# A hybrid attention, state-space and expert block: waits inside an expert pair taken out, and the second norm computed in another way

## The chip, the cores and the metric

The kernel runs on one core of one Trainium2 chip. The metric is the device time of one execution in microseconds (us), as the median of several runs. The profile was taken from one more execution of the same program.

## The reference, cut to what matters

256 tokens of width 2048 pass through a mixer (attention beside a state-space model), a layer norm, a mixture of 32 experts and a second layer norm. The change lies in the experts and in the second norm. Each token goes to its two best experts; all 32 experts are needed, and the weights of one are three matrices of 2048 x 512 numbers of 4 bytes.

```python
h = layer_norm(DEEPNORM_ALPHA * x + mix, ln1_g, ln1_b)
...
def expert_block(args):
    tok, e = args
    xb = h[tok]
    return (jax.nn.silu(xb @ w_gate[e]) * (xb @ w_up[e])) @ w_down[e]
...
out = jnp.zeros((n, d), jnp.float32).at[buf_tok].add(y.reshape(buf_len, d) * buf_w[:, None])
...
return layer_norm(DEEPNORM_ALPHA * h + ffn, ln2_g, ln2_b)

def layer_norm(x, g, b):
    mu = xf.mean(-1, keepdims=True)
    var = jnp.square(xf - mu).mean(-1, keepdims=True)
    return ((xf - mu) * lax.rsqrt(var + NORM_EPS) * g + b).astype(x.dtype)
```

## The kernel before, in words

The instructions of each engine stand in the order in which the code is written; nothing reorders them. The first 425 us hold the mixer, the first norm and the router. Then the experts follow, two at a time, in 16 pairs (0 to 15; the last is `LASTP`). Each expert has room for 64 tokens, and the two experts of a pair fill the two halves of TensorE's columns. Tokens beyond 64 for one expert would be treated in the overflow loop behind the pairs (`tc.For_i`), whose count comes from the data; with these inputs the profile shows no pass of it.

A pair does the following. TensorE multiplies the gathered tokens `xg` by the gate weights (`p_gate`) and the up weights (`p_up`), in four pieces each. `hidden` then lets ScalarE take the silu, VectorE multiply by the up half, TensorE transpose the result (`p_ht`) and ScalarE copy it into the tile `xg` (`aT`). `gather` makes the tokens of the next pair by matmuls with a one-hot matrix `S` (`p_g`); it has four parts. `weights_t` makes the routing weights of the pair (`p_sw`), which ScalarE copies to `swT` and `wsl`. The down products (`p_dn`) come in four chunks of 512 columns; `weighted` splits each into a high and a low part for the fast fp32r matmul (ScalarE writes the one, VectorE the other), and `combine` adds them to the sums of all tokens through a matmul with `swT` (`p_co`). In the last pair all weights come in half-size pieces and the down products in eight chunks of 256 columns.

Products in PSUM lie in banks that are used in turn by tag: "acc" has three, "s" and "t" two each, "o" one. `p_ht` and `p_sw` share "o"; `p_g` uses "t"; `p_dn` and `p_co` use "acc" (the last pair's `p_dn` uses "t").

The weights come through one queue of SyncE into a ring of slots, in program order. `ring_take` gives a piece to the matmuls and puts its slot on the list of free ones, and `ring_fill` writes loads into the free slots, oldest first; on the chip such a load waits until the matmuls that read the slot are done. A load also waits until the eighth load before it has landed, since there are eight DMA semaphores. Late in the program other tiles take slots from the same list.

`split_rows2` and `rows2` bring g and b of the second norm into two tiles whose 128 rows are all alike. Behind the overflow loop `norm_stats` aggregates the statistics, and `normed`, `scaled` and `shifted` apply the norm in eight units (two halves of the tokens by four column ranges), each followed by its store.

Of the kernel before, what the change touches and what calls it, by code (L numbers as in the profile page):

```python
# [10 lines left out]
F32 = mybir.dt.float32  # L11
# [59 lines left out]
def block_kernel(ctx: ExitStack, tc: tile.TileContext, I: dict, out: bass.AP):  # L71
# [878 lines left out]
    def ring_load(n=1):  # L950
        for i in range(ring["next"], min(ring["next"] + n, len(items))):
            nm, src, e, q = items[i]
            if second(i):
                at, t = ring["open"]
            else:
                at = ring["free"].pop(0)
                t = slot(at, "w" + nm)
                ring["open"] = at, t
            ring["next"] = i + 1
            ring["tiles"][nm, e, q] = t, at  # L960
            if nm == "row":
                nc.sync.dma_start(t[:8, :512], I["ln2_rows"])
# [185 lines left out]
    def weighted(py, wsl, i):  # L1148
# [4 lines left out]
        dve.scalar_tensor_tensor(lo, py, wsl, f(hi), op0=OP.mult, op1=OP.subtract)  # L1153
        return hi, lo

    def combine(swT, ys, lo, w, fin=None, init=False):
        s = slice(lo, lo + w)
        for a in range(2):
            pc = bank("acc", "p_co")[:, :w]
            for y, part in enumerate(ys):  # L1160
                pe.matmul(pc, swT[:, a * P:(a + 1) * P], part, start=(y == 0), stop=(y == 1))  # L1161
            if init:
                dve.tensor_copy(acc[a][:, s], pc)
            else:
                dve.tensor_add(acc[a][:, s], acc[a][:, s], pc)  # L1165
            if fin:
                for h in range(lo, lo + w, 256):
                    dve.bn_stats(st2[:, a, h // 256], acc[a][:, h:h + 256])

    def sums_first(lo, w):  # L1170

# [3 lines left out]
        return pcs  # L1175

    def combine_last(pcs, swT, ys, lo, w):
        for y, part in enumerate(ys):
            for a in range(2):
                pe.matmul(pcs[a], swT[:, a * P:(a + 1) * P], part, start=False, stop=(y == 1))  # L1180
# [73 lines left out]
        dve.tensor_scalar(base, base, float(P), float(CAP), op0=OP.mult, op1=OP.add)  # L1254


    gb = {}

    def split_rows2():

        raw = ring_take("row", -1, None)[:8, :512]
        gb["rows"] = mo.tile([64, 512], F32R, name="gb2", tag="gb1")
        gb["one"] = mo.tile([64, 8], F32R, name="one2")
        dve.memset(f(gb["rows"]), 0.0)
        dve.tensor_add(gb["one"], ident[:64, 0:8], ident[:64, 32:40])
        act.copy(gb["rows"][:8], raw)
        dve.tensor_tensor(gb["rows"][32:40], raw, f(gb["rows"][:8]), op=OP.subtract)

    def rows2(j):
        if j % 4 == 0:  # L1270
            gb[j // 4] = slot(ring["free"].pop(0), f"row{j // 4}")
        p = bank("acc", "p_row")
        pe.matmul(p, gb["one"][:40, j:j + 1].to_broadcast([40, P]), gb["rows"][:40], start=True, stop=True)
        act.copy(gb[j // 4][:, 512 * (j % 4):512 * (j % 4) + 512], p)

    st2 = mo.tile([P, 2, 8, 6], F32, name="st2")
    one_hots(0)
# [12 lines left out]
    for j in range(8):  # L1290
        besides.setdefault((LASTP, "g" if j < 2 else "u", (3, 3, 0, 0, 0, 1, 1, 1)[j]), []).append((rows2, j))
    for pr in range(NE // 2):
        pg, pu = bank("s", "p_gate"), bank("s", "p_up")
        for nm, pp in (("g", pg), ("u", pu)):
# [26 lines left out]
        aT = next(hid)  # L1321
        if pr < LASTP:
            weights_t(pr)
        late = None
        for i, (c, lo, w) in enumerate(DOWN_LAST if pr == LASTP else DOWN):
            tl = [ring_take("d", 2 * pr + u, (lo, w)) for u in range(2)]
            py = bank("t" if pr == LASTP else "acc", "p_dn")[:, :w]
            for q in range(4):
                for u in range(2):
                    pe.matmul(py[64 * u:64 * u + 64, :], aT[:, q, 64 * u:64 * u + 64], tl[u][:, q], start=(q == 0),  # L1330
                              stop=(q == 3), skip_group_check=True)
            ring_fill()
# [70 lines left out]
    mean, rstd, nmr = norm_stats(st2, "2")  # L1403
    dve.scalar_tensor_tensor(nmr, mean, -1.0, rstd, op0=OP.mult, op1=OP.mult)  # L1404
    units = [(a, slice(c * 512, (c + 1) * 512)) for a in range(2) for c in range(4)]

    def normed(i):
        a, s = units[i]
        act.activation(acc[a][:, s], acc[a][:, s], AF.Identity, scale=rstd[:, a:a + 1], bias=nmr[:, a:a + 1])

    def scaled(i):
        a, s = units[i]
        v = acc[a][:, s]
        if i % 2 == 0:
            dve.scalar_tensor_tensor(v, v, mean[:, a:a + 1], gb[0][:, s], op0=OP.subtract, op1=OP.mult)  # L1415
# [3 lines left out]
    def shifted(i):
        a, s = units[i]  # L1420
        v = acc[a][:, s]
        if i % 2 == 0:
            dve.scalar_tensor_tensor(v, v, rstd[:, a:a + 1], gb[1][:, s], op0=OP.mult, op1=OP.add)  # L1423
        else:
            pool.tensor_tensor(v, v, gb[1][:, s], op=OP.add)  # L1425

    def store(i):
        a, s = units[i]
        nc.sync.dma_start(out[0][a * P:(a + 1) * P, s], acc[a][:, s])

    for i in (1, 3, 5, 7):
        normed(i)
    for fn, i in ((scaled, 0), (shifted, 0), (scaled, 1), (shifted, 1), (scaled, 3), (shifted, 3), (scaled, 2), (scaled, 5),
                  (shifted, 5), (shifted, 2), (scaled, 7), (shifted, 7), (scaled, 4), (shifted, 4), (scaled, 6),
                  (shifted, 6)):
        fn(i)
# [10 lines left out]
def _laid_out(inputs):  # L1447
# [22 lines left out]
    a["ln2_rows"] = np.concatenate([flat("ln2_g"), flat("ln2_b")]).reshape(8, 512)  # L1470
# [22 lines left out]
```

## Time and profile before

| | |
|---|---|
| median of 3 runs | 1393.09 us (1392.07 to 1394.43) |
| the profiled execution: its own time | 1393.33 us |
| its span, first to last instruction | 1391.6 us |
| TensorE busy in the span | 94% |
| VectorE, ScalarE, GpSimd busy | 37%, 26%, 11% |
| read from HBM | 468.79 MB |

The span is 1.73 us shorter than the time of the execution it belongs to. Shares are means over stages with different limits, and TensorE's matmuls are pipelined, so that 94% doesn't say which engine or transfer sets the end of a stage.

### The profile page before, as it was taken

How to read it: one execution, taken by the hardware profiler on the slowest of the kernel's cores; microseconds unless marked ns; L12 is line 12 of the kernel's file. 1: busy time of each engine (PE TensorE's matmuls, PEld its weight loads, DVE VectorE, ACT ScalarE, POOL GpSimd, SP SyncE). 2: the span in 40 equal slices, each digit the busy share in tenths (PEclk: the TensorE clock that was granted, in tenths of full speed). 3: DMA queues.
4: the chain of work that ended last, by engine and by line, in shares of the span. 5: the costliest groups of instructions: out<-in, count | busy, mean ns of one | idle time of the engine just before them, and what ended most of it. 6: DMA issues, size and time to landing. Idle time of an engine off the chain costs nothing. (4 is left out here: it accounts for less than half of the span.)

```text
span 1391.6 us, 18135 instructions
## 1 busy us (share of the span) xinstructions
PE 1312.2 (94%) x7347; PEld 758.6 (55%) x7347; DVE 513.8 (37%) x1085; ACT 357.2 (26%) x687; POOL 154.1 (11%) x78
## 2 busy tenths in 40 slices
PE   7998999999999999999999999999999999999994
PEld 6778899997885434344344443444434444344432
DVE  6757676468833323131121312213122131221207
ACT  5554566455424102011010111101111011110112
POOL 2533233333520000000000000000000000000001
PEclk9999999999999999999999999999999999999997
DMA  8752334435798899999999999999999999999981
GB/s 314 288 177 91 122 103 141 152 122 212 302 412 342 350 391 421 421 421 421 421 421 421 421 421 421 421 421 421 421 421 421 421 421 421 421 420 421 407 325 61
DMA packets 70692, 472.10 MB, mean 339 GB/s; under 512 B 8510, under 2 KB 8766, under 8 KB 17102
## 3 DMA queue, kind: packets, MB, share of 16 engines
q1 hardware_dynamic: 70016, 470.75, 83.6%
q8 instruction: 59, 0.97, 0.3%
q10 hardware_dynamic: 590, 0.17, 0.1%
q14 instruction: 27, 0.22, 0.0%
HBM read 468.79 MB, written 2.10 MB: 338 GB/s over the span
## 5 line engine op out<-in xcount | busy, mean ns | idle before, releaser
L1330 PE MATMUL p_dn<-wd,xg 128*64 128x512 f32 (+1 forms) x1088 | 241.4, 587 | 14.9 <-DVE work L1153 14.3
L1300 PE MATMUL p_gate<-wg,xg 128*64 128x512 f32 x1024 | 225.9, 596 | 0.0
L1300 PE MATMUL p_up<-wu,xg 128*64 128x512 f32 x1024 | 222.9, 592 | 0.0
L222 POOL TENSOR_TENSOR w_lo<-raw,w_hi 128x1024 fp32r<-128x1024 f32 x52 | 141.4, 2721 | 258.4 <-ACT w_hi L221 245.8
L1189 DVE TENSOR_TENSOR xg<-xg,p_up 128x512 f32<-128x512 f32 x16 | 11.0, 688 | 394.1 <-ACT xg L1188 394.1
L1300 PEld LDWEIGHTS p_up<-wu,xg 128*64 128x64 f32 x1024 | 73.3, 137 | 145.5 <-issue 141.9
L1330 PEld LDWEIGHTS p_dn<-wd,xg 128*64 128x64 f32 x1088 | 73.7, 139 | 142.7 <-issue 108.0
L1300 PEld LDWEIGHTS p_gate<-wg,xg 128*64 128x64 f32 x1024 | 71.6, 137 | 143.7 <-issue 136.2
L1153 DVE SCALAR_TENSOR_TENSOR work<-p_dn,wsl,work 128x512 fp32r<-128x512 f32 (+1 forms) x68 | 48.9, 719 | 269.8 <-ACT work L1152 269.8
L1125 PEld LDWEIGHTS p_g<-S,hp 128*128 128x128 f32 x1024 | 120.8, 194 | 28.2 <-issue 26.0
L1125 PE MATMUL p_g<-S,hp 128*128 128x128 f32 x1024 | 127.2, 281 | 0.9 <-DVE cnt L1278 0.9
L221 ACT CAST w_hi<-raw 128x1024 fp32r<-128x1024 f32 (+1 forms) x112 | 109.0, 1027 | 36.9 <-issue 9.1
L1152 ACT ACTIVATE work<-p_dn,wsl 128x512 fp32r<-128x512 f32 (+1 forms) x68 | 45.2, 664 | 278.2 <-PE p_dn L1330 275.1
L1425 POOL TENSOR_TENSOR sum<-sum,row 128x512 f32<-128x512 f32 x4 | 6.7, 1691 | 972.3 <-DVE sum L1417 972.3
L310 PE MATMUL p_acc<-xh,w_hi 128*128 128x256 f32 x384 | 112.5, 293 | 0.0
L1188 ACT ACTIVATE xg<-p_gate 128x512 f32<-128x512 f32 x16 | 9.6, 597 | 391.7 <-PE p_up L1300 391.7
L312 PE MATMUL p_acc<-xl,w_hi 128*128 128x256 f32 x384 | 109.6, 285 | 0.0
L313 PE MATMUL p_acc<-xh,w_lo 128*128 128x256 f32 x384 | 109.6, 285 | 0.0
L222 DVE TENSOR_TENSOR w_lo<-raw,w_hi 128x1024 fp32r<-128x1024 f32 (+1 forms) x60 | 78.2, 1309 | 33.1 <-ACT w_hi L221 33.0
L1165 DVE TENSOR_TENSOR sum<-sum,p_co 128x512 f32<-128x512 f32 (+1 forms) x130 | 79.7, 650 | 9.5 <-PE p_co L1161 9.5
L1161 PE MATMUL p_co<-work,swT 128*128 128x512 f32 (+1 forms) x268 | 76.7, 408 | 0.0
L310 PEld LDWEIGHTS p_acc<-xh,w_hi 128*128 128x128 f32 x384 | 74.8, 195 | 0.7
(382 smaller groups left out, 1465.2 us busy)
## 6 DMA issues: line engine op xcount, KB each, us to landing
wg<-in_w_gate SPq DMA_DIRECT2D x120, 1024.0 KB, 15.3
wu<-in_w_up SPq DMA_DIRECT2D x120, 1024.0 KB, 17.7
wd<-in_w_down SPq DMA_DIRECT2D x120, 1024.0 KB, 11.7
raw<-in_w_dense SPq DMA_DIRECT2D x52, 1024.0 KB, 4.9
wg<-in_w_gate SPq DMA_DIRECT2D x16, 512.0 KB, 10.8
wu<-in_w_up SPq DMA_DIRECT2D x16, 512.0 KB, 10.2
wd<-in_w_down_last SPq DMA_DIRECT2D x16, 512.0 KB, 10.2
cw<-in_cmp_w SPq DMA_DIRECT2D x4, 1024.0 KB, 6.8
```

The source lines that it names most:

```text
L221: act.copy(hi[:, ks, :w], raw)
L222: eng.tensor_tensor(lo[:, ks, :w], raw, f(hi[:, ks, :w]), op=OP.subtract)
L310: pe.matmul(dst, hi[:, k, s], xk(xh, kt), start=(first and k == 0 and j % 2 == 0), stop=False, skip_group_check=True)
L312: pe.matmul(dst, hi[:, k, s], xk(xl, kt), start=False, stop=False, skip_group_check=True)
L313: pe.matmul(dst, lo[:, k, s], xk(xh, kt), start=False, stop=(last and k == 3), skip_group_check=True)
L1125: pe.matmul(at(k), hpm[a][:, 4 * c + k], S[:, a], start=(a == 0), stop=(a == 1))
L1152: act.activation(hi, py, AF.Copy, scale=wsl)
L1153: dve.scalar_tensor_tensor(lo, py, wsl, f(hi), op0=OP.mult, op1=OP.subtract)
L1161: pe.matmul(pc, swT[:, a * P:(a + 1) * P], part, start=(y == 0), stop=(y == 1))
L1165: dve.tensor_add(acc[a][:, s], acc[a][:, s], pc)
L1300: pe.matmul(pp[64 * u:64 * u + 64, :], xg[:, kk, 64 * u:64 * u + 64], tl[u][:, k], start=(kk == 0), stop=(kk == KT - 1), skip_group_check= ...
L1330: pe.matmul(py[64 * u:64 * u + 64, :], aT[:, q, 64 * u:64 * u + 64], tl[u][:, q], start=(q == 0), stop=(q == 3), skip_group_check=True)
```

## The change: what it does

Inside a pair, three things move or change place. `weights_t` of a pair is written into its up products (behind the second piece) instead of ahead of its down products. The transposes `p_ht` stand between the first two parts of the gather instead of behind them. The second and third down product use the banks "t" instead of "acc".

In the last pair the weighted down product is kept whole in fp32 (`weighted_whole`, no high and low part, one fp32 matmul instead of two fp32r ones), `g` is multiplied onto the sums as soon as each chunk is summed (`vg`), and the statistics, a small matmul (`p_rl`) and the rows `rowl` follow ahead of the overflow loop (`stats2`). Behind it, each unit of the norm is a matmul that makes -mean\*rstd\*g + b (`rows_in`), and one VectorE operation, `vg`\*rstd plus that; for three units TensorE also adds `vg`\*rstd (a fp32 matmul with a diagonal) and ScalarE copies the result. GpSimd has no part in it. The square root's function table is loaded by a small activation in the last pair. g and b are split in rows of 2048 in the last pair's gate products (`row_places`, `split_rows2`), where six tiles take ring slots. The count of the overflow loop is read into the engines' registers in pair 8.

```diff
+    def weighted_whole(py, wsl, i):
+        y = WK[0][:, 512 * (i % 2):512 * (i % 2) + py.shape[-1]]
+        act.activation(y, py, AF.Copy, scale=wsl)
+        return y,
...
             if fin:
                 for h in range(lo, lo + w, 256):
                     dve.bn_stats(st2[:, a, h // 256], acc[a][:, h:h + 256])
+                dve.tensor_mul(vg[a][:, s], acc[a][:, s], gb["g"][:, s])
...
+    def row_places():
+        t = slot(ring["free"].pop(0), "late")[:, :6 * P].rearrange("p (i a c) -> p i a c", i=3, a=2)
+        place, gb["cols"], gb["diag"] = [t[:, i] for i in range(3)]
...
     def split_rows2():
+        raw = ring_take("row", -1, None)
+        gb["rows"] = slot(ring["free"].pop(0), "gb2", F32R)
         dve.memset(f(gb["rows"]), 0.0)
+        for r, n in ((0, 2), (32, 2), (64, 1)):
+            act.copy(gb["rows"][r:r + n], raw[r:r + n])
+        dve.tensor_tensor(gb["rows"][32:34], raw[32:34], f(gb["rows"])[32:34], op=OP.subtract)
...
+        pe.matmul(p, gb["both"][:65], gb["rows"][:65, s], start=True, stop=True)
+        act.copy(gb["g"][:, s], p)
+
+    def stats2(between=None):
+
+        for a in range(2):
+            dve.bn_aggr(mv2[:, a], st2[:, a])
+        act.activation(rstd2, mv2[:, :, 1], AF.Sqrt, bias=epsc)
+        if between:
+            between()
...
+        for a in range(2):
+            dve.scalar_tensor_tensor(cols[:, a], place[:, 0], nmr2[:, a:a + 1], place[:, 1], op0=OP.mult, op1=OP.add)
+            pe.matmul(p[:, a * P:(a + 1) * P], cols[:, a], ident, start=True, stop=True)
+        act.copy(rowl[:65], p[:65])
+        dve.tensor_tensor(rowl[64:65], p[64:65], f(rowl)[64:65], op=OP.subtract)
+        for a in range(2):
+            act.activation(diag[:, a], ident, AF.Copy, scale=rstd2[:, a:a + 1])
...
-               (1, "u", 0): [(block_table,)], (LASTP, "u", 0): [(weights_t, LASTP)],
-               (LASTP - 1, "g", 0): [(split_rows2,)]}
+               (1, "u", 0): [(block_table,)], (8, "u", 2): [(count_blocks,)],
+               (LASTP, "g", 3): [(row_places,), (split_rows2,)]}
+    for pr in range(NE // 2):
+        besides.setdefault((pr, "u", 1), []).append((weights_t, pr))
...
         next(hid)
+        if pr == LASTP:
+            WK[0] = slot(WORK, "works")
+            act.activation(rstd2, ident[:, 0:2], AF.Sqrt, bias=epsc)
         if pr < LASTP:
             gather(xg, SEL[pr + 1], 0)
+        aT = next(hid)
+        if pr < LASTP:
             gather(xg, SEL[pr + 1], 1)
...
-            py = bank("t" if pr == LASTP else "acc", "p_dn")[:, :w]
+            py = bank("t" if pr == LASTP or i in (1, 2) else "acc", "p_dn")[:, :w]
...
+        pe.matmul(pn[a, c], gb["rowl"][:65, a * P:(a + 1) * P], gb["rows"][:65, s], start=True, stop=not by_act)
+        if by_act:
+            pe.matmul(pn[a, c], gb["diag"][:, a], vg[a][:, s], start=False, stop=True)
...
+        if (a, c) in BY_ACT:
+            act.copy(acc[a][:, s], pn[a, c])
         else:
+            dve.scalar_tensor_tensor(acc[a][:, s], vg[a][:, s], rstd2[:, a:a + 1], pn[a, c], op0=OP.mult, op1=OP.add)
```

ScalarE's order in one of the middle pairs, from the silu (`xg<-p_gate`) to the first part of the next pair's; first before, then in the change.

```order
L1188 ACTIVATE xg<-p_gate 128x512
L1129 ACTIVATE xg<-p_g,ln_127 128x128 x4
L1194 COPY xg<-p_ht 128x512
L1143 CAST swT<-p_sw 128x256
L1145 COPY wsl<-p_sw 64x1 x2
L1152 ACTIVATE work<-p_dn,wsl 128x512 x4
```

```order
L1144 CAST swT<-p_sw 128x256
L1146 COPY wsl<-p_sw 64x1 x2
L1195 ACTIVATE xg<-p_gate 128x512
L1201 COPY xg<-p_ht 128x512
L1130 ACTIVATE xg<-p_g,ln_127 128x128 x4
L1153 ACTIVATE work<-p_dn,wsl 128x512 x4
```

The copy of `p_ht`, for which the down products wait, now follows the silu at once, and the two copies of `p_sw` stand ahead of the silu.

TensorE's order in the last pair, from the gate products to the transposes; first before, then in the change, where `p_row` reads the tile `gb` that `split_rows2` writes (`rowl` also holds the selector `both`).

```order
L1300 MATMUL p_gate<-wg,xg 64x512 x32
L1273 MATMUL p_row<-gb_8127,one_8128 128x512 x2
L1300 MATMUL p_up<-wu,xg 64x512 x8
L1137 MATMUL p_sw<-ident,S 128x128 x2
L1139 MATMUL p_sw<-wt,S 128x2 x2
L1273 MATMUL p_row<-gb_8127,one_8128 128x512 x3
L1300 MATMUL p_up<-wu,xg 64x512 x8
L1273 MATMUL p_row<-gb_8127,one_8128 128x512 x3
L1300 MATMUL p_up<-wu,xg 64x512 x16
L1193 MATMUL p_ht<-ident,xg 128x128 x4
```

```order
L1353 MATMUL p_gate<-wg,xg 64x512 x32
L1353 MATMUL p_up<-wu,xg 64x512 x8
L1302 MATMUL p_row<-gb_8474,rowl 128x512
L1353 MATMUL p_up<-wu,xg 64x512 x8
L1138 MATMUL p_sw<-ident,S 128x128 x2
L1140 MATMUL p_sw<-wt,S 128x2 x2
L1302 MATMUL p_row<-gb_8474,rowl 128x512
L1353 MATMUL p_up<-wu,xg 64x512 x8
L1302 MATMUL p_row<-gb_8474,rowl 128x512
L1353 MATMUL p_up<-wu,xg 64x512 x8
L1302 MATMUL p_row<-gb_8474,rowl 128x512
L1200 MATMUL p_ht<-ident,xg 128x128 x4
```

Four row products in place of eight stand between the pieces of the up products, the last of them behind the last piece.

ScalarE's order at the same place in the change, from the gather of pair 14 on; before, the one split of g and b (L1266, 8x512) stood a pair earlier.

```order
L1130 ACTIVATE xg<-p_g,ln_127 128x128 x4
L1292 CAST gb_8474<-wrow 2x2048 x2
L1292 CAST gb_8474<-wrow 1x2048
L1303 COPY row<-p_row 128x512
L1144 CAST swT<-p_sw 128x256
L1146 COPY wsl<-p_sw 64x1 x2
```

Three copies of 2048 columns stand ahead of the first copy of a row product. The slot that `gb` takes is the one whose gate weights the last piece of the gate products reads.

## Rows read from the trace of the kernel before

**Rows 1.** The page, its 40 equal slices of the span: bytes moved by DMA.

```profile
GB/s 314 288 177 91 122 103 141 152 122 212 302 412 342 350 391 421 421 421 421 421 421 421 421 421 421 421 421 421 421 421 421 421 421 421 421 420 421 407 325 61
```

**Rows 2.** Waits of TensorE from 425 us on: total us, times, longest us.

```profile
PE p_sw L1137 <- ACT xg L1194: 24.0, 15, 1.6
PE p_dn L1330 <- DVE work L1153: 14.3, 30, 0.5
```

**Rows 3.** Timeline, pair 7 to 8 on TensorE: start us, us, engine, line, instructions, [idle before].

```profile
880.33 3.84 PE L1125 MATMUL p_g<-S,hp 128*128 128x128 f32 x32
...
886.25 0.44 PE L1137 MATMUL p_sw<-ident,S 128*128 128x128 f32 x2 [1.60 <-ACT xg L1194]
...
886.96 3.65 PE L1330 MATMUL p_dn<-wd,xg 128*64 128x512 f32 x16
...
897.78 3.65 PE L1330 MATMUL p_dn<-wd,xg 128*64 128x512 f32 x16 [0.47 <-DVE work L1153]
...
910.47 13.95 PE L1300 MATMUL p_gate<-wg,xg 128*64 128x512 f32 x64
...
924.25 13.90 PE L1300 MATMUL p_up<-wu,xg 128*64 128x512 f32 x64
```

**Rows 4.** Two stretches: us, busy us of each engine, then PEclk, DMA share, GB/s.

```profile
425.00:500.00 75.00, 71.91 (x376) 35.70 (x378) 25.32 (x68) 18.57 (x35) 0.00 (x0) 0.96 0.86 337
850.00:1290.00 440.00, 421.05 (x2150) 186.57 (x2149) 88.02 (x168) 56.21 (x130) 0.00 (x0) 1.00 1.01 421
```

**Rows 5.** Waits of SyncE's queue, from 425 to 505 us.

```profile
SPq L971 <- PE p_dn L1330: 17.5, 2, 12.8
```

**Rows 6.** The same view, from 1000 to 1345 us.

```profile
SPq L971 <- DMA wg<-in_w_gate: 86.3, 51, 2.2
```

**Rows 7.** Tile wu in pair 14: durations, first and last issue; time to landing.

```profile
L971 SPq DMA_DIRECT2D wu<-in_w_up x8: 327/328/328, 1234.3 to 1251.7; - x8
...
DMA to landing us min/median/max: 19.8/19.8/19.8
```

**Rows 8.** Tile wu in the last pair, the same columns.

```profile
L971 SPq DMA_DIRECT2D wu<-in_w_up x16: 327/328/328, 1303.0 to 1322.1; - x16
...
DMA to landing us min/median/max: 10.2/10.2/10.2
```

**Rows 9.** Timeline of TensorE at the last pair's end.

```profile
1340.59 7.09 PE L1300 MATMUL p_up<-wu,xg 128*64 128x512 f32 x32
...
1350.58 3.67 PE L1330 MATMUL p_dn<-wd,xg 128*64 128x256 f32 x32 [0.68 <-ACT xg L1194]
...
1357.40 1.95 PE L1330 MATMUL p_dn<-wd,xg 128*64 128x256 f32 x16
...
1367.58 1.95 PE L1330 MATMUL p_dn<-wd,xg 128*64 128x256 f32 x16
```

**Rows 10.** Groups by line and shape: line, engine, operation, count, busy us, mean ns of one.

```profile
L690 ACT ACTIVATE xbc<-xbc 128x2048 f32<-128x2048 f32 x2 | 3.8, 1918 | 0.0
...
L1267 DVE TENSOR_TENSOR gb<-wrow,gb 8x512 fp32r<-8x512 f32 x1 | 0.7, 680 | 0.7 <-ACT gb L1266 0.7
...
L1264 DVE MEMSET gb<- 64x512 f32 x1 | 0.5, 485 | 0.0
```

**Rows 11.** Timeline of TensorE in pair 14, behind the wait for `p_sw`.

```profile
1291.21 5.33 PE L1330 MATMUL p_dn<-wd,xg 128*64 128x512 f32 x16
```

**Rows 12.** The stretch of that row, columns as in rows 4.

```profile
1291.30:1294.60 3.30, 3.30 (x8) 0.91 (x10) 0.00 (x0) 0.57 (x3) 0.00 (x0) 0.50 1.05 412
```

**Rows 13.** Timeline of ScalarE and VectorE behind the last pair.

```profile
1372.51 0.70 ACT L1183 COPY sum<-p_co 128x256 f32<-128x256 f32 x2 [2.46 <-DVE st L1182]
...
1374.61 0.60 DVE L1016 BATCH_NORM_AGGREGATE mv<-st 128x2 f32<-128x48 f32 x2 [1.81 <-issue]
...
1379.10 1.75 DVE L1415 SCALAR_TENSOR_TENSOR sum<-sum,mv,row 128x512 f32<-128x512 f32 x1
...
1387.88 0.75 DVE L1423 SCALAR_TENSOR_TENSOR sum<-sum,rstd,row 128x512 f32<-128x512 f32 x1
```

More of the change, by code (lines that the diff above doesn't have):

```diff
@@ L1160, in combine @@
             for y, part in enumerate(ys):
-                pe.matmul(pc, swT[:, a * P:(a + 1) * P], part, start=(y == 0), stop=(y == 1))
+                pe.matmul(pc, (swT if len(ys) == 2 else f(swT))[:, a * P:(a + 1) * P], part, start=(y == 0),
+                          stop=(y == len(ys) - 1))
             if init:
@@ L1177, in combine_last @@
     def combine_last(pcs, swT, ys, lo, w):
-        for y, part in enumerate(ys):
-            for a in range(2):
-                pe.matmul(pcs[a], swT[:, a * P:(a + 1) * P], part, start=False, stop=(y == 1))
+        for a in range(2):
+            pe.matmul(pcs[a], f(swT)[:, a * P:(a + 1) * P], ys[0], start=False, stop=True)
         for a in range(2):
@@ L1257, in block_kernel @@
     gb = {}
+    vg = {}
+    mv2 = mo.tile([P, 2, 2], F32, name="mv2")
+    rstd2 = mo.tile([P, 2], F32, name="rstd2")
+    nmr2 = mo.tile([P, 2], F32, name="nmr2")
+    def row_places():
+        t = slot(ring["free"].pop(0), "late")[:, :6 * P].rearrange("p (i a c) -> p i a c", i=3, a=2)
+        place, gb["cols"], gb["diag"] = [t[:, i] for i in range(3)]
+        gb["place"] = place
+        t = slot(ring["free"].pop(0), "rowl", F32R)
+        gb["rowl"], both = t[:, :T], t[:, T:T + P]
+        gb["both"] = both
+        dve.memset(place, 0.0)
+        for r in (0, 32, 64):
+            dve.memset(place[:, 0, r:r + 1], 1.0)
+        for r in (1, 33):
+            dve.memset(place[:, 1, r:r + 1], 1.0)
+        dve.memset(f(both), 0.0)
+        for r in (0, 32):
+            dve.memset(f(both)[r:r + 1], 1.0)
@@ L1269, in rows2 @@
+        dve.tensor_tensor(gb["rows"][32:34], raw[32:34], f(gb["rows"])[32:34], op=OP.subtract)
     def rows2(j):
-        if j % 4 == 0:
-            gb[j // 4] = slot(ring["free"].pop(0), f"row{j // 4}")
+        if j == 0:
+            gb["g"] = slot(ring["free"].pop(0), "row")
+            for a in range(2):
+                vg[a] = slot(ring["free"].pop(0), f"vg{a}")
         p = bank("acc", "p_row")
-        pe.matmul(p, gb["one"][:40, j:j + 1].to_broadcast([40, P]), gb["rows"][:40], start=True, stop=True)
@@ L1274, in rows2 @@
-        act.copy(gb[j // 4][:, 512 * (j % 4):512 * (j % 4) + 512], p)
+        s = slice(512 * j, 512 * j + 512)
+        pe.matmul(p, gb["both"][:65], gb["rows"][:65, s], start=True, stop=True)
[6 more added lines that the diff above has]
+            between()
+        dve.reciprocal(rstd2, rstd2)
+        dve.scalar_tensor_tensor(nmr2, mv2[:, :, 0], -1.0, rstd2, op0=OP.mult, op1=OP.mult)
+        p = bank("t", "p_rl")[:, :T]
+        place, cols, diag, rowl = [gb[n] for n in ("place", "cols", "diag", "rowl")]
+        for a in range(2):
+            dve.scalar_tensor_tensor(cols[:, a], place[:, 0], nmr2[:, a:a + 1], place[:, 1], op0=OP.mult, op1=OP.add)
+            pe.matmul(p[:, a * P:(a + 1) * P], cols[:, a], ident, start=True, stop=True)
+        act.copy(rowl[:65], p[:65])
+        dve.tensor_tensor(rowl[64:65], p[64:65], f(rowl)[64:65], op=OP.subtract)
+        for a in range(2):
+            act.activation(diag[:, a], ident, AF.Copy, scale=rstd2[:, a:a + 1])
@@ L1289, in block_kernel @@
         besides[j, "g", 2] = [(residual, j, 1)]
-    for j in range(8):
-        besides.setdefault((LASTP, "g" if j < 2 else "u", (3, 3, 0, 0, 0, 1, 1, 1)[j]), []).append((rows2, j))
+    for j in range(4):
+        besides.setdefault((LASTP, "u", j), []).append((rows2, j))
     for pr in range(NE // 2):
@@ L1341, in block_kernel, with last_vg @@
         else:
-            combine_last(sums_first(*late[2:4]), *late[:4])
+            pcs = sums_first(*late[2:4])
+            combine_last(pcs, *late[:4])
+            s = slice(late[2], late[2] + late[3])
+            def last_vg():
+                for a in range(2):
+                    dve.tensor_mul(vg[a][:, s], pcs[a], gb["g"][:, s])
+            stats2(last_vg)
         SW.pop(pr)
     OVER = ring["free"][:4]
-    nblk = nc.values_load(tabi[0:1, 8:9], min_val=0, max_val=NBLK)
     ov = mw
-    with tc.For_i(0, nblk, 1) as b:
+    WK[0] = slot(WORK, "oworks", F32R)
+    with tc.For_i(0, gb["n"], 1) as b:
         e = nc.values_load(tabi[0:1, bass.ds(b, 1)], engines=[mybir.EngineType.SP], min_val=0, max_val=NE - 1)
@@ L1400, in block_kernel @@
             combine(swT, ys, 512 * c, 512, True)
[L1403 to L1415, printed above, removed]
-        else:
-            dve.tensor_mul(v, v, gb[0][:, s])
@@ L1419, in shifted @@
[L1419 to L1436, printed above, removed]
@@ L1437, in block_kernel, with store, rows_in @@
-    for i in (0, 1, 3, 2, 5, 4, 7, 6):
-        store(i)
+        stats2()
+    def store(a, s):
+        nc.sync.dma_start(out[0][a * P:(a + 1) * P, s], acc[a][:, s])
+    BY_ACT = ((0, 2), (1, 1), (1, 3))
+    tags = iter(["acc"] * 3 + ["s"] * 2 + ["t"] * 2 + ["o"])
+    pn = {}
+    def rows_in(a, c):
+        pn[a, c] = bank(next(tags), "p_n")
+        s = slice(512 * c, 512 * c + 512)
+        by_act = (a, c) in BY_ACT
+        pe.matmul(pn[a, c], gb["rowl"][:65, a * P:(a + 1) * P], gb["rows"][:65, s], start=True, stop=not by_act)
+        if by_act:
+            pe.matmul(pn[a, c], gb["diag"][:, a], vg[a][:, s], start=False, stop=True)
@@ L1441 @@
+    order = ((0, 0), (0, 2), (0, 1), (1, 1), (0, 3), (1, 0), (1, 3), (1, 2))
+    for a, c in order:
+        rows_in(a, c)
+    for a, c in order:
+        s = slice(512 * c, 512 * c + 512)
+        if (a, c) in BY_ACT:
+            act.copy(acc[a][:, s], pn[a, c])
+        else:
+            dve.scalar_tensor_tensor(acc[a][:, s], vg[a][:, s], rstd2[:, a:a + 1], pn[a, c], op0=OP.mult, op1=OP.add)
+    for a, c in order:
+        store(a, slice(512 * c, 512 * c + 512))
 _INS = ['x', 'positions', 'w_in', 'cmp_k_pe', 'cmp_k_w1', 'cmp_k_b1', 'cmp_k_w2', 'cmp_v_pe', 'cmp_v_w1',
```

18 lines of the change are left out of this document (6 added, 12 removed).

## The prediction, made before the changed kernel was run

> **What bounds the kernel now.** I read the slices of the page first. From slice 15 on (from about 520 us) DMA moves 421 GB/s in every slice up to the end of the loads [rows 1]; the reader should see a flat line where the work of a pair goes up and down, so something steady sets it. The stretches say the same: DMA share 1.01 at 421 GB/s from 850 to 1290 us, but 0.86 at 337 GB/s from 425 to 500 us [rows 4]. The queue's own waits tell why: in the early stretch it stands waiting for matmuls to free slots (up to 12.8 us at once) [rows 5], later for the landing of earlier loads [rows 6]. So from 500 us on the weights come as fast as the transfers go. A pair has 24 loads of 1.05 MB, 25.2 MB, and takes 59.8 us at that rate.
>
> Next, the timeline of a pair on TensorE [rows 3]. From the first gather matmul behind one pair's up products (880.33) to the end of the next pair's (924.25 + 13.90 = 938.15) is 57.8 us. TensorE is thus the faster of the two, by 2 us a pair, and lives on a lead of the weights. The waits view names no wait for a load from 425 us on; its two big rows are 24.0 us over 15 times for `p_sw` behind the copy of `p_ht`, and 14.3 us over 30 times for `p_dn` behind VectorE [rows 2]. TensorE sets the end, but the lead is nearly used up: the last up weights are issued at 1322.1 and land 10.2 us later, at 1332.3 [rows 8]; the up products end at 1340.59 + 7.09 = 1347.7 [rows 9]. One piece, an eighth, of them takes 1.7 us (13.9 / 8), so with perfect TensorE they could end at 1334.1. **At most 13.6 us of TensorE's time can be taken out ahead of that point,** unless the weights come sooner too.
>
> **The change, part by part.**
>
> *Middle pairs.* The wait of 1.60 us goes: the down products need the copy of `p_ht`, and the second gather part (half of 3.84 us) now covers it [rows 3]. The work of `p_sw` (886.25 to 886.96, 0.7 us) only moves into the up products. The two waits of 0.47 us go, since the third and fourth product find a bank that VectorE has left; I add nothing for the pipeline's refill there. That is 2.5 to 2.8 us a pair; I take 2.6. New hazards: the second down product takes the bank that ScalarE empties behind the second gather part, but a whole down product (3.65 us) lies between. Over 15 pairs, 39 us, three times the 13.6 us there is room for; the rest becomes waiting for weights in the later pairs.
>
> *The weights themselves.* Up to 500 us the loads wait for slots that pair 0 frees, and its down products free them 1.6 to 2.6 us sooner. Behind that the stream is full. So the whole stream moves forward by up to 2.6 us, at least by nothing; I take 2.6, as the waits of [rows 5] are for just these matmuls.
>
> *The last pair, up to the end of the up products.* Pair 14's last up weights land at 1251.7 + 19.8 = 1271.5 [rows 7], now 1268.9; a piece of 3.5 us makes 1272.5. From there to the next gate product took 30.1 us (880.33 to 910.47); less 2.6 and the moved 0.7 it is 26.8, so the last gate products start at 1299.3 and end, 13.9 us on, at 1313.2 [rows 3]. Their last piece frees the slot that the split rows take. Only then comes the chain of `split_rows2`: a memset of 2048 columns, four times the 485 ns for 512, 1.9 us; two copies of 2048 columns on ScalarE, 1.9 us each by the row of that width; a subtraction, four times 680 ns, 2.7 us [rows 10]; with hand-overs 8.7 us (the third copy runs beside the subtraction). The first row product stands behind two pieces of the up products, at 1316.7 on TensorE, and must wait until 1321.9. This is a new wait of 5.2 us, and the other six pieces are queued behind it: 10.4 us, 0.7 for `p_sw`, 0.9 for row products, to 1333.9. A bound from below is the weights' (1329.7 + 1.8 = 1331.5), had the rows been ready.
>
> *The clock.* Behind the 1.6 us wait in pair 14 the granted clock was 0.50, that is 1.2 GHz, for a stretch [rows 12], and the down product took 5.33 instead of 3.65 us [rows 11, 3]. A 5.2 us idle should do it at least once: +1.7 us (bounds 0 and 3.4). The up products end at 1335.6, 12.1 us sooner than before. The Trainium skill (TensorE: Matmul & The Clock Gate, "HAM oscillation — how this bites in real kernels") says that waits for DMA in a matmul loop halve the clock again and again. The trace agrees for one wait [rows 12]. By it the waits for weights in the later pairs would each cost some clock; what that makes here is the last rival.
>
> *Behind the up products.* One row copy stands ahead of the silu on ScalarE, +0.8 us on the 2.9 us from 1347.7 to the down products at 1350.58 [rows 9]; the table load hides beside VectorE's multiply and the transposes. Down products: chunks come every 2.54 us ((1367.58 - 1357.40) / 4). A fp32 matmul of 128 columns is two instructions of 0.12 us (3.84 / 32), so two of 256 columns take 0.96 us; the four fp32r ones of one instruction each, 0.48. So +0.45 us a chunk, +2.7 for six; VectorE's part of a chunk (two sums, two statistics, two products, near 0.4 us each) stays under 3.0 us. The eighth chunk starts 19.7 us behind the first, at 1359.0, not 1367.6.
>
> *Tail.* It took 1391.6 - 1367.6 = 24.0 us. Now VectorE has to finish chunks seven and eight (5.6 us behind the eighth's start) and run the statistics, the two products, `p_rl` and the row split, 3.5 us, some ten short steps at 0.2 to 0.4 us; together 9.1. Then the loop's entry: from ScalarE's last copy (1373.21) to the aggregate was 1.4 us [rows 13], for TensorE I take 0.8. The eight row matmuls and three fp32 ones are 4.3 us at full clock; TensorE has idled for 5 us, so I count a first part at half clock, 6.0 us. Last VectorE operation 0.75, hand-over 0.2, then as before 3.0 us from the end of the last operation (1387.88 + 0.75) to the span's end. Sum 19.8 (bounds: 18.2 at full clock, 22.4 all at half). GpSimd's absence is in this: VectorE's operations of 0.75 us took 1.75 beside it [rows 13].
>
> **The sum.** 1359.0 + 19.8 = 1378.8 us of span, 12.8 less than 1391.6: up products -12.1, silu +0.8, chunks +2.7, tail -4.2. With the 1.73 us around the span, 1380.5; the profiled run lies 0.24 us over the median, so **1380**.
>
> **Rivals.**
>
> *The rows are ready in time.* If the slot is free sooner or copies of two rows are short, the up products end at the weights' bound with no fall of the clock, 4.1 us sooner; with a full-clock tail 1.6 more: 1374.3. Against it: the order, and copies whose price goes by columns. Chance 0.17.
>
> *A dearer end.* The stream comes no sooner (+2.6), a second stretch at 1.2 GHz in the last pair (+1.7), the tail all at half clock (+2.6): 1387. Chance 0.10.
>
> *Waits count in full.* If the 421 GB/s were set by TensorE's demand, 15 times 2.6 us and the tail come off: about 1352. Against it: loads that wait for landings, not slots [rows 6]. Chance 0.03.
>
> *The waits move.* If the copy of `p_ht` or a bank still holds TensorE at another place, pairs keep 57.8 us, the last pair pays +3.5 and the tail gives 4.2: 1392, no change. The table of banks speaks against it. Chance 0.04.
>
> *Slower: the clock stays down.* If TensorE, waiting for weights, were held at 1.2 GHz through the last pair's up and down products, their 33 us would double: some 1410. It decides from 16 us lost, half of that work. For it: the fall in [rows 12]. Against: an engine that is slowed stops waiting for weights, and the stretch of [rows 12] was followed by full clock. This is where the rule of the Trainium skill's page above would end if it held throughout. Chance 0.03.
>
> **Numbers.** The likeliest case, 0.62, gives 1375 to 1385; with the first two rivals the range is 1371 to 1387. About 0.2% (2.8 us) is what a measurement here can tell from no change. Faster by more: 0.93; within: 0.04; slower: 0.03.
>
> **What would show it.** Pairs near 55.2 us at first (those without residual work), later ones at 59.8 with TensorE waiting for loads; `p_row` behind VectorE or ScalarE for about 5 us in the last pair; the last up weights landing near 1330; down chunks 3.0 us apart; a norm of about 8 us behind the loop with TensorE at 0.50 in its first part. Wrong it would be if DMA in the middle left 421 GB/s, or if `p_row` never waits.

## The result, and the profile after

| | before | after |
|---|---|---|
| median (range) of 4 runs each, us | 1393.76 (1392.07 to 1395.85) | 1384.82 (1384.54 to 1385.32) |
| profiled execution: time, span, us | 1393.33, 1391.6 | 1384.74, 1383.0 |

The ratio is 0.9936, with a 95% interval from 0.9918 to 0.9953. The changed kernel is faster by 8.9 us; the prediction said 1380.0, in 1371 to 1387. In spans the gain is 8.6 us and not the 12.8 of the sum. Where the 4.2 us went is the question of this part.

The waits of TensorE from 420 us on, in the changed kernel, columns as in [rows 2]:

```profile
PE p_up L1353 <- DMA wu<-in_w_up: 15.5, 13, 1.3
PE p_row L1302 <- DVE gb L1293: 5.1, 1, 5.1
PE p_rl L1318 <- DVE late L1317: 2.8, 1, 2.8
PE p_ht L1200 <- DVE xg L1196: 2.7, 2, 1.9
PE p_n L1478 <- ACTq L1412: 1.7, 1, 1.7
```

The 24.0 and 14.3 us of [rows 2] are gone. TensorE now waits for up weights 13 times, and once for the split rows. The stretches of the changed kernel, columns as in [rows 4]:

```profile
900.00:1090.00 190.00, 182.92 (x903) 83.68 (x901) 34.87 (x66) 23.14 (x54) 0.00 (x0) 1.00 1.01 421
...
1321.10:1327.60 6.50, 6.50 (x17) 1.88 (x17) 0.00 (x0) 0.59 (x1) 0.00 (x0) 0.59 1.02 409
1340.10:1345.40 5.30, 5.26 (x33) 2.96 (x33) 0.00 (x0) 0.47 (x1) 0.00 (x0) 0.68 0.91 362
1371.00:1379.00 8.00, 7.81 (x14) 4.19 (x14) 2.98 (x5) 1.48 (x3) 0.00 (x0) 0.59 0.38 145
```

The middle runs at 421 GB/s and full clock, waits and all. The other three stretches are at the end, and in each the granted clock (the number after the last bracket) is partly 0.50, that is 1.2 GHz. The timeline of TensorE shows what they cost; columns as in [rows 3]:

```profile
883.85 13.95 PE L1353 MATMUL p_gate<-wg,xg 128*64 128x512 f32 x64
...
939.12 13.95 PE L1353 MATMUL p_gate<-wg,xg 128*64 128x512 f32 x64
...
1312.36 3.60 PE L1353 MATMUL p_up<-wu,xg 128*64 128x512 f32 x16
1321.10 0.77 PE L1302 MATMUL p_row<-gb,rowl 65*128 65x512 f32 x1 [5.14 <-DVE gb L1293]
1321.79 5.93 PE L1353 MATMUL p_up<-wu,xg 128*64 128x512 f32 x16
...
1332.73 3.65 PE L1353 MATMUL p_up<-wu,xg 128*64 128x512 f32 x16
...
1338.71 0.75 PE L1200 MATMUL p_ht<-ident,xg 128*128 128x128 f32 x4 [1.90 <-DVE xg L1196]
1340.13 5.31 PE L1385 MATMUL p_dn<-wd,xg 128*64 128x256 f32 x32 [0.68 <-ACT xg L1201]
...
1346.43 1.95 PE L1385 MATMUL p_dn<-wd,xg 128*64 128x256 f32 x16
...
1361.12 1.95 PE L1385 MATMUL p_dn<-wd,xg 128*64 128x256 f32 x16
...
1371.07 1.22 PE L1478 MATMUL p_n<-gb,rowl 65*128 65x512 f32 x2 [1.74 <-ACTq L1412]
...
1378.09 0.79 PE L1478 MATMUL p_n<-gb,rowl 65*128 65x512 f32 x1
```

Behind the 5.14 us wait two pieces take 5.93 us where later ones take 3.65; the first down products take 5.31 where [rows 9] had 3.67; the norm's matmuls last from 1371.07 to 1378.9. The chain that the row products waited for, on VectorE and ScalarE:

```profile
1313.03 1.76 DVE L1290 MEMSET gb<- 128x2048 f32 x1 [1.48 <-PE p_gate L1353]
1314.83 5.72 ACT L1292 CAST gb<-wrow 2x2048 fp32r<-2x2048 f32 x3 [15.59 <-DVE gb L1290]
1318.67 2.28 DVE L1293 TENSOR_TENSOR gb<-wrow,gb 2x2048 fp32r<-2x2048 f32 x1 [3.87 <-ACT gb L1292]
```

Three copies of one or two rows take 1.9 us each, as long as one of 128 rows in [rows 10]: their price goes by columns. The last up weights answer to [rows 8]; issue ends at 1318.8 instead of 1322.1:

```profile
L972 SPq DMA_DIRECT2D wu<-in_w_up x16: 327/328/328, 1299.7 to 1318.8; - x16
...
DMA to landing us min/median/max: 10.1/10.2/10.2
```

### The profile page after: what moved, and what is told of

It is laid out like the page before. It is cut to its first block, busy times and chain, and to the rows that moved or that the text cites. A ratio compares the mean times of both kernels' runs of the same rounds, so it can differ in the third digit from the quotient of the medians.

```text
span 1383.0 us, 18200 instructions
## 1 busy us (share of the span) xinstructions
PE 1330.1 (96%) x7361; PEld 771.8 (56%) x7361; DVE 512.2 (37%) x1097; ACT 361.7 (26%) x688; POOL 147.3 (11%) x74
## 5 line engine op out<-in xcount | busy, mean ns | idle before, releaser
L1353 PE MATMUL p_up<-wu,xg 128*64 128x512 f32 x1024 | 241.8, 600 | 15.5 <-DMA wu<-in_w_up 15.5
L1385 PE MATMUL p_dn<-wd,xg 128*64 128x512 f32 (+1 forms) x1088 | 236.2, 577 | 0.7 <-ACT xg L1201 0.7
L1353 PEld LDWEIGHTS p_up<-wu,xg 128*64 128x64 f32 x1024 | 83.5, 138 | 156.0 <-issue 113.9
L1154 DVE SCALAR_TENSOR_TENSOR work<-p_dn,wsl,work 128x512 fp32r<-128x512 f32 x60 | 45.1, 751 | 203.8 <-ACT work L1153 203.8
L1153 ACT ACTIVATE work<-p_dn,wsl 128x512 fp32r<-128x512 f32 x60 | 41.3, 688 | 225.6 <-PE p_dn L1385 223.5
L1144 ACT CAST swT<-p_sw 128x256 fp32r<-128x256 f32 x16 | 6.0, 372 | 332.4 <-PE p_sw L1140 332.4
L312 PEld LDWEIGHTS p_acc<-xl,w_hi 128*128 128x128 f32 x384 | 74.3, 193 | 0.0
L313 PEld LDWEIGHTS p_acc<-xh,w_lo 128*128 128x128 f32 x384 | 74.2, 193 | 0.0
## 6 DMA issues: line engine op xcount, KB each, us to landing
wg<-in_w_gate SPq DMA_DIRECT2D x120, 1024.0 KB, 19.8
wu<-in_w_up SPq DMA_DIRECT2D x120, 1024.0 KB, 19.8
wd<-in_w_down SPq DMA_DIRECT2D x120, 1024.0 KB, 19.8
wu<-in_w_up SPq DMA_DIRECT2D x16, 512.0 KB, 10.2
wd<-in_w_down_last SPq DMA_DIRECT2D x16, 512.0 KB, 10.2
```

The costliest lines, as they stand in the source:

```text
L312: pe.matmul(dst, hi[:, k, s], xk(xl, kt), start=False, stop=False, skip_group_check=True)
L313: pe.matmul(dst, lo[:, k, s], xk(xh, kt), start=False, stop=(last and k == 3), skip_group_check=True)
L1153: act.activation(hi, py, AF.Copy, scale=wsl)
L1353: pe.matmul(pp[64 * u:64 * u + 64, :], xg[:, kk, 64 * u:64 * u + 64], tl[u][:, k], start=(kk == 0), stop=(kk == KT - 1), skip_group_check= ...
```

## The experiments

The theory: the pair part brings the kernel down to the pace of the weights, and the norm part, as placed, gives some of it back in the last pair: a wait for the split rows, dearer down products, and a clock that falls behind each idle stretch. The rivals: TensorE still sets the middle; or the new norm carries part of the gain. Measured beside the experiments, the kernel before had medians between 1392.5 and 1393.0 us.

| run | median, us (range) | ratio to before, 95% |
|---|---|---|
| e1 pair part alone | 1380.18 (1375.78 to 1381.34) | 0.9909 (0.9894 to 0.9924) |
| e2 norm part alone | 1401.49 (1400.58 to 1403.05) | 1.0064 (1.0050 to 1.0078) |
| e3 changed, more TensorE work | 1386.68 (1385.82 to 1387.29) | 0.9953 (0.9939 to 0.9966) |
| e4 before, the same work | 1423.73 (1422.75 to 1427.22) | 1.0220 (1.0205 to 1.0234) |
| e5 row products later | 1381.22 (1378.10 to 1381.57) | 0.9908 (0.9894 to 0.9922) |
| e6 down products split | 1385.46 (1382.49 to 1389.89) | 0.9951 (0.9937 to 0.9965) |
| e7 idle time filled | 1386.94 (1386.42 to 1387.73) | 0.9957 (0.9944 to 0.9970) |
| e8 = e5 + e7 | 1384.61 (1380.51 to 1385.18) | 0.9936 (0.9923 to 0.9948) |
| e9 = e7, code shifted | 1387.11 (1386.33 to 1388.76) | 0.9958 (0.9944 to 0.9972) |
| e10 norm on VectorE alone | 1383.15 (1382.66 to 1386.75) | 0.9935 (0.9922 to 0.9949) |
| e11 = e5 + e6 + e10 | 1377.56 (1373.13 to 1377.65) | 0.9889 (0.9872 to 0.9905) |
| e12 = e5 + e10 | 1379.53 (1378.76 to 1380.80) | 0.9904 (0.9888 to 0.9921) |

### The two halves of the change: e1 and e2

In e1, the kernel before gets the pair part, and nothing else:

```diff
+    for pr in range(LASTP):
+        besides.setdefault((pr, "u", 1), []).append((weights_t, pr))
...
             gather(xg, SEL[pr + 1], 0)
+        aT = next(hid)
+        if pr < LASTP:
             gather(xg, SEL[pr + 1], 1)
...
+            py = bank("t" if pr == LASTP or i in (1, 2) else "acc", "p_dn")[:, :w]
```

> The kernel before with the pair part alone: p_sw in the up products, p_ht between the first two gather parts, the second and third down product in the other banks. Row products, split of g and b, last pair's down products and norm as before. Theory (the middle's TensorE time is taken out until the weights set the pace, and what stands behind the up products costs as before): last up weights land near 1329, up products end near 1331 to 1332 in place of 1347.7, and the 43.9 us behind them stay; 1376 to 1379 us. That is less than the whole change (1384.8), so the norm part as placed would give back some 7 us. Rival (the norm part carries part of the gain): 1387 to 1390. Second rival (the pair part only moves the waits): 1392 to 1394.

e2 is the changed kernel with these lines as they were.

> The changed kernel with the pairs ahead of the last one arranged as before (p_sw ahead of the down products, both gather parts ahead of p_ht, all down products in the acc banks). Theory: TensorE sets the end, so the wait for the split rows (5.1), the fall of the clock behind it (2.5), the silu's place (0.8), the fp32 products (2.7) and the clock at the first down products (1.6) all count in full, against a tail some 2 us shorter and four row products fewer (0.9): 1398 to 1402 us, slower than before. Rival (the new norm is worth its 4 us, and the wait for the rows hides): 1388 to 1391.

The pair part alone is 12.3 us faster than before, the norm part alone 9.0 us slower: e2 fell inside what the theory gave, and e1 came 1.2 us above it. Both rivals fell: that the norm carries part of the gain, and that the pair part only moves the waits. The two halves do not add up: on top of the pair part the norm part costs 4.6 us by the medians, and not 9.0. In e1's timeline:

```profile
1321.59 8.29 PE L1302 MATMUL p_up<-wu,xg 128*64 128x512 f32 x32
...
1332.78 3.67 PE L1331 MATMUL p_dn<-wd,xg 128*64 128x256 f32 x32 [0.68 <-ACT xg L1194]
...
1350.03 1.95 PE L1331 MATMUL p_dn<-wd,xg 128*64 128x256 f32 x16
```

The up products end at 1329.9 us, 6.5 ahead of the changed kernel's 1336.4, and the granted clock is 1.00 from 430 to 1354 us, so no fall touches its last pair. (This execution is e1's shortest, at a mean clock of 0.992; its other three had 0.988 or 0.989.) In e2 the wait of 5.1 us stands in full, and its first down products took 6.43 us.

### Who sets the pace of the middle: e3 and e4

```diff
-                    for u in range(2):
+                    for u in [0, 1] * (3 if nm == "g" and kk == 0 and 0 < pr < LASTP else 1):
```

> The changed kernel with the first four gate matmuls... of pairs 1 to 14 done three times: the first gate matmul of each of the two experts is repeated twice, 4 more matmuls of 0.217 us a pair, 12.2 us in all; the result is the same, since each starts its sum anew. Theory (in the changed kernel the weights set the pace and TensorE has room to spare): the waits for up weights (15.5 us) shrink by most of 12 us and the time grows by at most 1.5: 1385 to 1386.5 us. Rival (TensorE still sets the end): 12 us more, 1397.

> The kernel before with the same 12.2 us of repeated gate matmuls in pairs 1 to 14. Theory (before, TensorE sets the end and the weights wait for nothing of it): 12 us more, 1405 to 1406 us. Rival (the stream of weights already sets the end before): within 2 us of 1393.

I had mis-sized the added work: the timeline counts two instructions for each of these fp32 matmuls, and the gate products of a pair rose from 13.95 to 15.67 us, so that 14 pairs have 24.1 us more. The wait for up weights in e3, columns as in [rows 2]:

```profile
PE p_up L1353 <- DMA wu<-in_w_up: 2.4, 2, 1.2
```

The gate products of a pair in e4's timeline:

```profile
923.82 15.67 PE L1300 MATMUL p_gate<-wg,xg 128*64 128x512 f32 x72
```

The changed kernel swallows 24.1 us for 1.9: 13.1 of it took the place of waits for weights (15.5 less 2.4); the other 9 or so I take to have come out of the lead that TensorE wins in the earlier pairs (up to 900 us the changed kernel has no wait for weights), but no row separates them. The kernel before pays more than all: 31.2. Behind the wait for `p_sw`, which is 1.60 us in every pair, the first down product took 5.3 us instead of 3.65 in ten pairs of e4, and in four of the kernel before ([rows 11] is one of them). Six more by 1.7 are 10.2 us, and with the 24.1 that makes 34.3, where the profiled spans differ by 33.8. TensorE set the end before, the weights set the pace after.

### The wait for the rows: e5

```diff
-        besides.setdefault((LASTP, "u", j), []).append((rows2, j))
+        besides.setdefault((LASTP, "u", (1.5, 2, 2.5, 3)[j]), []).append((rows2, j))
```

> The changed kernel with the four row products behind the fifth to eighth eighth-piece of the last up products in place of the second, fourth, sixth and eighth; nothing else. Theory (the wait of 5.1 us for the split rows and the fall of the clock behind it hold TensorE while the weights are already there): no wait for the rows, up products end near 1331.5 instead of 1336.4, the whole 4 to 5.5 us sooner: 1379 to 1381 us. Rival (the weights arrive too late for it, or the clock falls elsewhere): 1383.5 to 1385.

3.6 us sooner than the changed kernel's median: the theory held, 0.2 us above what it gave. TensorE in e5:

```profile
1322.68 1.93 PE L1353 MATMUL p_up<-wu,xg 128*64 128x512 f32 x6 [0.21 <-DMA wu<-in_w_up]
...
1337.18 0.75 PE L1200 MATMUL p_ht<-ident,xg 128*128 128x128 f32 x4 [1.90 <-DVE xg L1196]
1338.60 3.67 PE L1385 MATMUL p_dn<-wd,xg 128*64 128x256 f32 x32 [0.68 <-ACT xg L1201]
```

No row product waits, a 0.21 us wait for weights is back, and the first down products run at full clock. This execution's loads began 2.4 us later than those of the changed kernel's profiled one (349.9 against 347.5 us), so its positions stand later than the median says. Its up products end at 1334.9, 1.5 us sooner than in the changed kernel, though its last up load was issued 3.9 us later (1322.7) and landed 10.2 us after that, one piece ahead of this end: here the weights set it.

### The down products: e6

```diff
-            ys = (weighted_whole if pr == LASTP else weighted)(py, SW[pr][1], i)
+            ys = weighted(py, SW[pr][1], i)
...
-            pe.matmul(pcs[a], f(swT)[:, a * P:(a + 1) * P], ys[0], start=False, stop=True)
+                pe.matmul(pcs[a], swT[:, a * P:(a + 1) * P], part, start=False, stop=(y == 1))
```

> The changed kernel with the last pair's weighted down products split into a high and a low part for two fp32r matmuls, as before, instead of one fp32 matmul; g is still multiplied early. Theory (each chunk's fp32 matmul costs 0.4 us more on TensorE, which is in line there): chunks 2.54 us apart, 2 to 3 us sooner: 1382 to 1383. Rival (VectorE, with two sums, two statistics, two products and the low part, sets the chunks): chunks 2.9 to 3.0 apart, no change: 1384 to 1386.

The chunks come 2.55 us apart, as the theory said, and VectorE is no bound there:

```profile
1345.62 1.95 PE L1386 MATMUL p_dn<-wd,xg 128*64 128x256 f32 x16
1347.50 0.74 PE L1167 MATMUL p_co<-works,swT 128*128 128x256 f32 x4
1348.17 1.95 PE L1386 MATMUL p_dn<-wd,xg 128*64 128x256 f32 x16
```

The profiled span, 1380.8, is 2.2 us less than the changed kernel's. But the median is 0.6 us higher, with runs that spread over 7.4 us; by itself e6 settles nothing of the whole. e11 against e12 does.

### The clock: e7, e8 and e9

```diff
+    def warm(tag, n):
+        p = bank(tag, "p_w")
+        for _ in range(n):
+            pe.matmul(p[:, :256], ident, acc[0][:, 0:256], start=True, stop=True)
...
+            warm("t", 3)
             WK[0] = slot(WORK, "works")
...
+            warm("o", 5)
             stats2(last_vg)
+            warm("o", 2)
```

> The changed kernel with idle TensorE filled by matmuls whose result nobody reads: three 128x256 ones behind the last up products, five behind the last sums, two behind p_rl. Theory (the first down products and the norm's matmuls run at 1.2 GHz because TensorE idled just ahead): the first two down products take 3.7 instead of 5.3 us, the norm's matmuls about 5 instead of 7.8, the end comes 3 to 4.5 us sooner: 1380 to 1382. Rival (the clock there comes from something else, or the norm's end is set by VectorE's and ScalarE's operations): at most 1 us sooner, 1384 to 1385.

> The row products later and the filling matmuls together. Theory (the two losses lie behind one another on TensorE's path and add): 7 to 9.5 us less than the changed kernel, 1375 to 1378. Rival (one hides behind the other): like the better of the two alone, 1379 to 1382.

Both missed: e7 came 2 us above its rival's range too, and e8, at 1384.6, 3.4 us above e5. TensorE in e7:

```profile
1338.74 0.75 PE L1200 MATMUL p_ht<-ident,xg 128*128 128x128 f32 x4 [0.60 <-DVE xg L1196]
1340.16 3.67 PE L1391 MATMUL p_dn<-wd,xg 128*64 128x256 f32 x32 [0.68 <-ACT xg L1201]
...
1373.51 1.22 PE L1486 MATMUL p_n<-gb,rowl 65*128 65x512 f32 x2 [4.92 <-issue]
```

The first filling did what it should: with the idle of 1.90 us ahead of the transposes cut to 0.60, the first down products take 3.67 us instead of 5.31. One execution would not show it, since e5 had 3.67 without filling; but of the kernels with the early row products, the two filled ones (e7, e9) took 3.67 and the five unfilled ones (the changed kernel, e2, e3, e6, e10) 5.29 to 6.43. But then TensorE stood 4.92 us ahead of the norm for no wait. The jumps of the overflow loop say why; their row on TensorE's sequencer in the view of the loop's line (min, median and max ns, first and last start), of the changed kernel:

```profile
L1412 PEldq COMPARE_BRANCH  x3: 101/187/398, 1368.9 to 1370.8; - x3
```

And of e7, the same view:

```profile
L1420 PEldq COMPARE_BRANCH  x3: 97/196/3572, 1367.3 to 1373.3; - x3
```

One jump took 3.57 us instead of at most 0.40. It began at 1368.8; a load of 16 KB on the instruction queue began inside it (1369.7), and another behind its end (1373.1). The changed kernel has one such load, behind its short jump (1370.6). I took it for a matter of where the code lies, and shifted it:

```diff
+    for pr in (11, 12):
+        besides[pr, "u", 1] = [(warm, "o", 5, P)]
```

> The kernel of the filling matmuls (e7) with ten more 128x128 matmuls that nobody reads, five each in the up products of pairs 11 and 12, where TensorE waits for weights anyway. They do no work at the end; they shift where TensorE's later instructions lie in its code. In e7 TensorE stood 4.9 us with no wait ahead of the norm's matmuls, and the trace has two loads of 16 KB on the instruction queue just there (at 1369.7 and 1373.1 us), where the changed kernel had one (1370.6). Theory (the jump out of the overflow loop met a load of code under way and needed another behind it; that the filling shifted the code is what cost e7 its gain): one load there, at most 2 us of standing, 2.5 to 5 us less than e7's 1386.9: 1382 to 1384.5. Rival (the filling itself holds up the entry to the loop): as e7, 1386 to 1388.

It missed, and 1387.1 lies in the rival's range. Two loads again, and a long jump:

```profile
L1422 PEldq COMPARE_BRANCH  x3: 101/196/3732, 1369.3 to 1375.4; - x3
```

That this jump held up the tail is shown, by the rows above; that it comes from where the code lies is not, and what in the filling makes it slow stays open (the filling behind `p_rl` was not tried without the rest). So no run had the norm's matmuls at full clock throughout, and none measures what the clock costs in the tail.

### The tail's matmuls: e10

```diff
-    BY_ACT = ((0, 2), (1, 1), (1, 3))
+    BY_ACT = ()
```

> The changed kernel with all eight units of the second norm made by VectorE: the three fp32 matmuls with the diagonal, and ScalarE's three copies, are gone. Theory (TensorE's 7.8 us of matmuls at 1.2 GHz set the tail): eight row matmuls of 0.46 us take under 4 us; VectorE, eight times 0.75 us from 1371.9 on, sets the end at about 1378, 1.5 to 2 us sooner: 1382.5 to 1383.5. Rival (VectorE is the bound of the tail, and the three units on ScalarE are a gain): no change or up to 1 us slower, 1385 to 1386.

1.7 us sooner; the theory held. Behind the loop, first TensorE and then VectorE:

```profile
1371.96 3.78 PE L1478 MATMUL p_n<-gb,rowl 65*128 65x512 f32 x8 [1.75 <-ACTq L1412]
...
1372.80 5.36 DVE L1490 SCALAR_TENSOR_TENSOR sum<-vg,rstd,p_n 128x512 f32<-128x512 f32 x8 [1.72 <-PE p_n L1478]
```

Eight row matmuls take 3.78 us at 1.2 GHz, half of the 7.8 that they took together with the fp32 ones, and VectorE, gapless, sets the end.

### What is worth keeping together: e11 and e12

> The changed kernel with the row products later (e5), the last pair's down products split as before (e6) and all units of the norm on VectorE (e10). Theory (three losses one behind the other on the path: wait and clock in the up products 3.6 us, fp32 products 2.2 by the profile of e6, fp32 matmuls of the tail 1.7): 7 to 8 us less than the changed kernel's 1384.8, 1376 to 1378.5, and less than the pair part alone (1380.2). Rival (the split is worth nothing, as the median of e6 says): 1379 to 1380.

> As e11, but with the down products whole in fp32. Theory: e5's 1381.2 less 1.7, 1379 to 1380, and 2 to 3 us above e11, by 0.4 us a chunk. Rival (the split is worth nothing): the same as e11 within 1 us.

Their edits are those shown. e11 is 15.4 us faster than before, and the best of all; by the medians it is 7.3 faster than the change, but 0.8 of that may be the measurements', since the kernel before stood at 1393.76 us beside the change and at 1392.97 beside e11; e12, without the split, is 2.0 us slower than e11, at the lower end of what was expected. So the split is worth its 2 us on the path. Two rows of e12's timeline show that the clock is not settled by the code alone:

```profile
1334.02 1.10 PE L1200 MATMUL p_ht<-ident,xg 128*128 128x128 f32 x4 [1.90 <-DVE xg L1196]
1335.79 6.24 PE L1385 MATMUL p_dn<-wd,xg 128*64 128x256 f32 x32 [0.68 <-ACT xg L1201]
```

The same code behind the same 1.90 and 0.68 us of idle, and with no wait for the rows ahead of it in either, took 3.67 us in e5.

## Why the prediction was right, and what its sum missed

*Weights behind a small lead.* Right, and shown by e3 against e4. The middle stays at 421 GB/s; early pairs take 55.3 us (883.85 to 939.12; 55.2 predicted), and the waits for weights are those foreseen. The rival in which all 39 us count fell with e1 and e3.

*The stream comes sooner.* The last up loads were issued 3.3 us sooner (2.6 taken). But the first loads of different executions lie up to 3.6 us apart (346.3 us in e11, 349.9 in e5), and the changed kernel's began 1.1 us sooner (347.5 against 348.6), ahead of the experts, where the change starts. Counted from the first load, 2.2 us are left, and 0.7 to 2.3 in the other runs with the pair part and no added gate matmuls: the sign is right, and the 2.6 was the upper bound.

*The wait for the split rows.* 5.14 us at 1321.10; predicted 5.2, to 1321.9. It began and ended 0.7 to 0.8 us sooner. The rival "rows ready in time" is what e5 built: 4.1 us sooner was its price, 3.6 the median's.

*Silu and chunks.* From the last up products to the down products 3.75 us (2.9 + 0.8 predicted); chunks 2.94 us apart (2.99). Both right; e11 against e12 has 2.0 us for the fp32 products, where the sum had 2.7 and the chunks of e6 give 2.3 (six times 0.39).

*The clock: the step that was mis-sized.* The sum had one fall for 1.7 us in the up products, and a part of the norm. There were three:

- Up products: 5.93 us for 3.65 and 0.77 for 0.50, 2.6 us in place of 1.7. The pieces and row products at full clock took 0.7 us more than the sum had, and the wait ended 0.8 sooner, which hides one of the two errors: the end came at 1336.4, 0.8 later than predicted.
- First down products: 5.31 for 3.67, 1.6 us that the sum did not have; the eighth chunk started 21.0 instead of 19.7 us behind the first. In [rows 9] this place was at full clock behind 1.48 us of idle, and I kept that though the idle there grew to 1.90 and the 5.2 us wait stood newly ahead. The filling took it away, by less idle time ahead (0.60). Neither of the two is shown to bring it by itself: behind 1.90 us of idle and without the 5 us wait it was gone in e5 and e11 and there in e12.
- Norm: 7.8 us of matmuls instead of 6.0. From the eighth chunk to the loop's end it took 9.95 us (9.9 predicted), and the tail 21.9 (19.8), near the upper bound of 22.4. That all of the 1.8 us is clock rests on the granted 0.59 of that stretch; e10 shows only that these matmuls set the end.

0.8 + 1.3 + 2.1 = 4.2 us, the whole miss in the span. The second fall in the last pair and the slow tail (2.1 us of the 2.6 there) are two of the three terms of the rival *A dearer end*, to which I gave 0.10; only the other, a stream that comes no sooner, stayed away. That the time still lies in the range of the likeliest case, 1375 to 1385, by 0.2 us, is luck.

One premise was weaker than it read. [rows 11] and [rows 12] show one of the 15 waits for `p_sw` in the kernel before, each of 1.60 us. Behind them the first down product took 3.65 us eleven times, as in [rows 3], and 5.33 to 5.35 four times. So the length of an idle stretch did not tell whether the clock falls, and a fall should have been priced by a chance at each place.

*The slower rival.* The clock did not stay down: the 13 waits for weights, none above 1.3 us, lie between 900 and 1320 us, and the granted clock is 1.00 from 430 to 1319 us. The Trainium skill (TensorE: Matmul & The Clock Gate, "HAM oscillation — how this bites in real kernels") tells of a matmul loop in which each wait for DMA, of about 3 to 5 us, is followed by a fall of the clock. No wait for weights here is that long, so no run tests it for them; the one wait that is, 5.14 us for VectorE, was followed by a fall. The wait in which the prediction saw the trace agree was 1.60 us for a copy on ScalarE ([rows 2]).

What the prediction did not see as one thing is that the norm part loses: I priced its steps, but never its sum against the old norm. Its own numbers had it: wait 5.2, clock 1.7, silu 0.8 and chunks 2.7 against 4.2 won in the tail. Beside the pair part it is less, since the weights alone would have held the up products to 1331.5: by the sum 4.1 + 0.8 + 2.7 - 4.2 = 3.4 us, and 4.6 was measured (e1).

## What to carry to other kernels

Split a change with two purposes before judging it: here 12.3 us won hid a half that alone lost 9.0, and of the 4.6 us by which the whole lies above its pair part, one position in an order is 3.6 (e5). Once the weights set the pace, as here, time taken out of the engine is worth nothing until the end, and each microsecond of serial work behind the last load counts in full. Where a wait is added ahead of a serial end, price the clock at each following idle stretch, not once, and with a chance, since the same idle brought a fall in some places and none in others.

## What the runs showed of the hardware

- Behind idle of the same length the clock falls at some places and in some executions, and not in others. Within one execution of the kernel before, behind the same 1.60 us, the first down product took 3.65 us in eleven pairs and 5.33 to 5.35 in four. Behind 1.90 and 0.68 us the first down products of the last pair took 3.67 (e5), 5.31 (changed kernel), 6.24 (e12) and 6.43 us (e2). Executions of e1 and e11 differ by some 4 us, with mean clocks of 0.992 and 0.993 in the shortest ones and near 0.989 in the others.
- A jump of TensorE's sequencer took 3.57 to 3.73 us in the three filled kernels, with a load of 16 KB on the instruction queue begun inside it, and at most 0.40 us in the changed kernel, where that load began behind it. Which of the two is the cause is not shown.
- A copy of one or two rows of 2048 columns took 1.9 us on ScalarE, as long as one of 128 rows in [rows 10].
